# A fourth block of 32 rows in the stacked parts of x and B of the samples' state update

## The chip, the cores and the metric

The kernel runs on one core of one Trainium2 chip. A core has a matrix engine (TensorE; in profiles PE for its matmuls and PEld for its loads of the stationary operand), a vector engine (VectorE, DVE), a scalar engine (ScalarE, ACT), GpSimd (POOL) and a queue engine (SyncE, SP). They run side by side and wait for each other through semaphores. Matmuls write to PSUM, a small memory that VectorE and ScalarE empty. The metric is device time in microseconds, as the median of several runs.

## The reference

One decoder layer on a prompt of 1024 rows and on 8 samples of 8 rows each (64 rows), at model width 1024. What matters here is the recurrent branch of the samples. Each of the 8 samples has a state h for each of 32 heads, 64 x 128 numbers, which is decayed over its 8 rows and gets what these rows add:

```python
def step(h, inp):
    xq, dq, Bq, Cq = inp
    acs = jnp.cumsum(dq * Ag, axis=1)
    ...
    last = acs[:, -1]
    w_in = jnp.exp(last[:, None] - acs) * dq
    h = h * jnp.exp(last)[..., None, None] + jnp.einsum('bjgn,bjge,bjgep->bgepn', Bq, w_in, xq)
    return h, y
```

The sum over j runs over the 8 rows of a sample alone. Heads come in 4 groups of 8; B is shared within a group. All of it is float32.

## The kernel before

The kernel first normalises, then projects the 1088 rows to all columns, 128 columns at a time, with seven products for a pair of column blocks in place of eight (Strassen's scheme). In a product (`product`, L614) two halves of 272 rows are summed over 12 matmuls each; the first half goes to a PSUM buffer of the pool named mm or ps, the second to the other pool, in turn. There are three buffers mm, four buffers ps and one pc. The weights are split into a rounded high part and the rest: ScalarE makes `whi` (L165), GpSimd `wlo` (L168). Results are gathered in s, u and c: the first product of a pair is copied out of PSUM by ScalarE (L655, s<-mm and s<-ps), the others are added by VectorE (L623, L628, of which u<-s,mm and u<-s,ps at L623 start a new u). The finished sums go through an activation (L730, u<-u, with its table of functions loaded where the one before was another) and are stored to DRAM from ScalarE's queue (L732, for instance gp<-u); a new u reuses the buffer of the old one when its store has landed.

Between the last ten pairs of these projections the state work of the samples is done, written as the generator `all_samples` over the four head groups. For group g:

- `begin` loads the group's x, B and C of the samples (xb, tile hst) and the decay table (dec). `decay` masks dec on GpSimd (`far`, L1201 and L1202) and takes its exponentials on ScalarE (`exps`, L1207, eight instructions of 64 x 64).
- `rows` turns x and multiplies dec with C and B (L1255, L1257 on TensorE; L1259 and L1261 on VectorE).
- `spread` and `split` prepare one half hf of the samples (4 samples, 32 rows). `spread` copies the 32 columns of each of four x blocks and of B side by side, as often as there are blocks of 32 rows (`rep`, L1268, GpSimd). `split` turns them (L1279, L1281), so that 32 rows come out stacked several times, and makes of the stack parts of x and of B: x is weighted with wd3 (L1283) and rounded (L1288), and on rows 64:96 the rounded part is taken off the exact one (L1289); B is rounded (L1291), the rest stands on rows 32:64 (L1292), and the result is spread over four samples with the mask blk3 (L1293). Summed over the stack, the three blocks give high x high, high x low and low x high.
- `turn`, `turned` and `state` turn the old states (L1309, emptied by L1314 as hT and yt) and multiply them with C (L1323, on tiles of 32 columns).
- `update` sums over the stack, for two heads and four samples at once (L1332, 32 matmuls in all with 512 columns), and adds the decayed old state on VectorE (L1335); the new state is stored from ScalarE's queue (L1337, out<-h).
- `out` and `end` gather the samples' output (L1342, L1347, L1349, L1353) and store it (L1355, ys<-xd).

wd3 comes from a small product in `dt_end` (L1168, L1169) with a selector sel3 that repeats 32 rows (L1161).

The order of TensorE's instructions in this stage is kept as written (`in_line`). VectorE, ScalarE, GpSimd and SyncE get theirs from a scheduler that places instructions by its own costs; each engine then takes its queue strictly in that order, stores included. PSUM buffers are handed out in the same pass, so which operation frees the buffer that a product gets can change with the order.

Of the kernel before, what the change touches and what calls it, by code (L numbers as in the profile page):

```python
# [8 lines left out]
F32 = mybir.dt.float32  # L9
F32R = mybir.dt.float32r  # L10
AF = mybir.ActivationFunctionType
ALU = mybir.AluOpType
# [8 lines left out]
P = 128  # L21
# [4 lines left out]
NS = 64  # L26
T = SEQ + NS
DI = 2048
NH = 32
# [4 lines left out]
NC = SEQ // CH  # L34
# [12 lines left out]
def tile_pool_ssd_step(  # L47
# [6 lines left out]
    nc = tc.nc  # L54
    uid = [0]

    def nm(s):
        uid[0] += 1
        return f"{s}_{uid[0]}"
# [37 lines left out]
    def PB():  # L97
        return psB.tile([P, 512], F32, tag="ps", name=nm("ps"))

    def PA():  # L100
        return psA.tile([P, 512], F32, tag="mm", name=nm("mm"))
# [5 lines left out]
    def const(shape, name, dt=F32):  # L107
        return cp.tile(shape, dt, tag=name, name=name)
# [3 lines left out]
    mm = nc.tensor.matmul  # L112
    act = nc.scalar.activation
    V = nc.vector


    ident = const([P, P], "ident")
# [44 lines left out]
    def split(raw, kept=None, ncols=P, eng=None):  # L162
        hi = wp.tile([P, 4, P], F32R, tag="whi", name=nm("whi"), bufs=4)
        lo = wp.tile([P, 4, P], F32R, tag="wlo", name=nm("wlo"), bufs=4)
        ins = act(hi[:, :, :ncols], raw[:, :, :ncols], AF.Copy)  # L165
        if kept is not None:
            kept.append(ins.ins)
        (eng or nc.gpsimd).tensor_tensor(lo[:, :, :ncols], raw[:, :, :ncols], hi[:, :, :ncols].bitcast(F32), ALU.subtract)  # L168
        return hi, lo
# [4 lines left out]
    def prep(src, nk):  # L174
        out = []
        with tc.high_priority(PRI):
            for k0 in range(0, nk, 4):
                raw = raw_()
                load(raw, src[k0 * P:(k0 + 4) * P, :].rearrange("(k p) c -> p k c", p=P))
                out.append(split(raw))  # L180
        return out
# [347 lines left out]
    def pair_w(c0, c1, pri, early, second):  # L529
        def run():  # L530
# [9 lines left out]
            def add(x):  # L540
                with tc.high_priority(pri):
                    w.append(split(x, highs, eng=V if early else None))
# [326 lines left out]
    def first():  # L869
# [12 lines left out]
        def w_split(t, j, eng=None):  # L882
            w[t, j] = split(raws[t, j], eng=eng)
# [198 lines left out]
    def dt_end():  # L1082
# [4 lines left out]
        nc.gpsimd.affine_select(maskS, maskS, [[8, NB], [1, 8]], ALU.is_ge, 0.0, base=0, channel_multiplier=-1)  # L1087
        nc.gpsimd.affine_select(maskS, maskS, [[-8, NB], [0, 8]], ALU.is_ge, 0.0, base=0, channel_multiplier=1)
        nc.gpsimd.tensor_copy(blkS.rearrange("p (b i) -> p b i", i=8), blk.unsqueeze(2).to_broadcast([NS, NB, 8]))
        for rr in range(3):  # L1090
            nc.gpsimd.tensor_copy(blk3[32 * rr:32 * rr + 32], blk[:32, 0:4])
        F = 9 * NH
# [8 lines left out]
        def tmp(tag, bufs):  # L1101
            return sp.tile([P, 512], F32, tag=tag, name=nm(tag), bufs=bufs)[:, :F]
# [4 lines left out]
        for c0 in (0, 4, 8):  # L1107
            ps = PB()
# [3 lines left out]
            for c in cs:  # L1112
                n = P if c < 8 else NS
# [5 lines left out]
        r, e, q, s2, p = tmp("xd", 2), tmp("xw", 1), tmp("h0", H0B), tmp("h0", H0B), tmp("hT", 1)  # L1119
# [18 lines left out]
        a = q  # L1138
# [15 lines left out]
        for n, f in ((P, slice(0, 256)), (NS, slice(256, F))):  # L1154
# [1 line left out]
            V.tensor_tensor(wd[:n, f], pt[:n, f], ac[:n, f], ALU.subtract)  # L1156
            act(wd[:n, f], wd[:n, f], AF.Exp, scale=-1.0)
            V.tensor_tensor(wd[:n, f], wd[:n, f], dt[:n, f], ALU.mult)
        sel3 = sp.tile([NS, 2, 3, 32], F32, tag="hst", name="sel3", bufs=2)
        for hf in range(2):  # L1160
            nc.gpsimd.tensor_copy(sel3[:, hf], ident[:NS, 32 * hf:32 * hf + 32].unsqueeze(1).to_broadcast([NS, 3, 32]))  # L1161
        wdt = wdT[:NS, 8, :]
        act(Elb.rearrange("p c h -> p (c h)"), pt[:, :256], AF.Exp, scale=-1.0)
        yield
        yield
        ps = PB()
        for hf in range(2):
            mm(ps[:96, hf * NH:(hf + 1) * NH], sel3[:, hf].rearrange("p r i -> p (r i)"), wdt, start=True, stop=True)  # L1168
        V.tensor_copy(wd3.rearrange("p a h -> p (a h)"), ps[:96, :2 * NH])  # L1169
        for c0 in range(0, 9, 4):  # L1170
            cs = range(c0, min(c0 + 4, 9))
            n = sum(P if c < 8 else NS for c in cs)
            ps = PB()
# [51 lines left out]
    def spt(shape, tag, bufs, dt=F32):  # L1225
        return sp.tile(list(shape), dt, tag=tag, name=nm(tag), bufs=bufs)

    class Samples:
# [34 lines left out]
        def spread(self, hf):  # L1263

            xb = self.xb
            rep = spt([P, 5, 2, 3, 16], "xw", 1).rearrange("p q a r i -> p q (a r i)").rearrange(
                "p q (r i) -> p q r i", i=32)
            nc.gpsimd.tensor_copy(rep, xb[:, 0:5, 32 * hf:32 * hf + 32].unsqueeze(2).to_broadcast([P, 5, 3, 32]))  # L1268
            cz = spt([P, 4, 32], "cz", 2)
            V.memset(cz, 0.0)  # L1270
            V.tensor_copy(cz[:, :, 0:8], xb[:, 5, 32 * hf:32 * hf + 32].rearrange("p (b i) -> p b i", i=8))
            self.half[hf] = rep, cz

        def split(self, hf):
            g = self.g
            rep, cz = self.half[hf]
            px = PB()
            for q in range(4):
                nc.tensor.transpose(px[:96, q * P:(q + 1) * P], rep[:, q].rearrange("p r i -> p (r i)"), ident)  # L1279
            pb = PB()  # L1280
            nc.tensor.transpose(pb[:96, :P], rep[:, 4].rearrange("p r i -> p (r i)"), ident)  # L1281
            xs = spt([P, 8, 64], "xw", 1)
            V.tensor_tensor(xs[:96], px[:96].rearrange("p (h d) -> p h d", d=64),  # L1283
                            wd3[:, hf, 8 * g:8 * g + 8].unsqueeze(2).to_broadcast([96, 8, 64]), ALU.mult)
            both = spt([P, 2, 512], "dec", 2, F32R)
            xh, Bb = both[:, 0], both[:, 1].rearrange("p (b n) -> p b n", n=P)
            xsf = xs.rearrange("p h d -> p (h d)")
            act(xh[:96], xsf[:96], AF.Copy)  # L1288
            V.tensor_tensor(xh[64:96], xsf[64:96], xh[64:96].bitcast(F32), ALU.subtract)  # L1289
            bx = spt([P, P], "bt", 1, F32R)  # L1290
            act(bx[:96], pb[:96, :P], AF.Copy)  # L1291
            V.tensor_tensor(bx[32:64], pb[32:64, :P], bx[32:64].bitcast(F32), ALU.subtract)  # L1292
            V.tensor_tensor(Bb[:96], bx[:96].bitcast(F32).unsqueeze(1).to_broadcast([96, 4, P]),  # L1293
                            blk3.unsqueeze(2).to_broadcast([96, 4, P]), ALU.mult)
            self.half[hf] = xh, Bb, cz

        def within(self):
# [28 lines left out]
        def update(self, j):  # L1326

            g, (hf, r), E2 = self.g, divmod(j, 4), self.E2
            xh, Bb, cz = self.half[hf]
            h0 = self.h0.pop(j)  # L1330
            pu = PB()
            mm(pu, xh[:96, r * P:(r + 1) * P], Bb[:96].rearrange("p b n -> p (b n)"), start=True, stop=True)  # L1332
            for b in range(4):
                cc_ = 32 * hf + 8 * b + 7
                V.scalar_tensor_tensor(h0[:, b, :], h0[:, b, :], E2[:, r, cc_:cc_ + 1],  # L1335
                                       pu[:, b * P:(b + 1) * P], ALU.mult, ALU.add)
            store_(new_ssm_s[0, 4 * hf:4 * hf + 4, 8 * g + 2 * r:8 * g + 2 * r + 2]  # L1337
                   .rearrange("b h p n -> (h p) b n"), h0)
# [126 lines left out]
    hst = [None] * NG  # L1465
# [156 lines left out]
    def to_ssd():  # L1622
        nonlocal right, sd, sp, mask, maskS, blkS, dtT, acT, wdT, wd3, blk3, Elb
        right.__exit__(None, None, None)
        sd_cm = tc.tile_pool(name="sd", bufs=1, side="right", reuse_waits="tile")
        sd = sd_cm.__enter__()
        right_all.append(sd_cm)

        def one(shape, name):
            return sd.tile(shape, F32, tag=name, name=name, bufs=1)  # L1630
        mask, maskS, blkS = one([P, P], "mask"), one([NS, NB, 8], "maskS"), one([NS, NS], "blkS")
        dtT, acT, wdT = one([P, 9, NH], "dtT"), one([P, 9, NH], "acT"), one([P, 9, NH], "wdT")
        wd3, blk3, Elb = one([96, 2, NH], "wd3"), one([96, 4], "blk3"), one([P, NC, NH], "Elb")
        right = tc.tile_pool(name="sp", bufs=2, side="right", reuse_waits="tile")
        sp = right.__enter__()
        dt_steps.append(dt_end())
        next(dt_steps[0])
# [13 lines left out]
    pre = splits()  # L1651
    units.append(plain(lambda: [None for _ in pre]))
    units.append(plain(to_ssd))
    acc = [None] * 8
    yh, yl = [None] * NG, [None] * NG
# [234 lines left out]
    ps = PB()  # L1890
    for c in range(9):
        n = min(P, T - c * P)
# [5 lines left out]
    for c in range(9):  # L1898
        n = min(P, T - c * P)
# [144 lines left out]
    px, py, pz = PA(), PA(), PA()  # L2044
# [183 lines left out]
```

## Time and profile before

| what | value |
|---|---|
| runs | 1265.39, 1267.29, 1271.7 us |
| median of 3 | 1267.29 us |
| span of the profiled execution (first to last instruction; the only time given for it) | 1265.2 us |
| TensorE busy, matmuls / loads | 1239.8 us (98%) / 1158.1 us (92%) |
| VectorE, ScalarE, GpSimd busy | 77%, 54%, 57% |
| mean granted TensorE clock | 0.999 |
| TensorE's waits from 540 to 790 us, where the changed lines run | 2.0 us |

A row of a group in the profile reads: line, engine, operation, output<-inputs, shapes, count, then busy time in us and the mean duration of one in ns, then the engine's idle time just before these instructions and what ended it. For matmuls the shapes are rows*columns of the stationary operand and then the moving operand. In a timeline a row is start, duration, engine (a q behind it means its queue, for instance a DMA issue), line, operation, count, and in brackets the idle time ahead of it with its cause.

### The profile page before, as it was taken

How to read it: one execution, taken by the hardware profiler on the slowest of the kernel's cores; microseconds unless marked ns; L12 is line 12 of the kernel's file. 1: busy time of each engine (PE TensorE's matmuls, PEld its weight loads, DVE VectorE, ACT ScalarE, POOL GpSimd, SP SyncE). 2: the span in 40 equal slices, each digit the busy share in tenths (PEclk: the TensorE clock that was granted, in tenths of full speed). 3: DMA queues.
4: the chain of work that ended last, by engine and by line, in shares of the span. 5: the costliest groups of instructions: out<-in, count | busy, mean ns of one | idle time of the engine just before them, and what ended most of it. 6: DMA issues, size and time to landing. Idle time of an engine off the chain costs nothing.

```text
span 1265.2 us, 26432 instructions
## 1 busy us (share of the span) xinstructions
PE 1239.8 (98%) x9679; PEld 1158.1 (92%) x9679; DVE 974.4 (77%) x1713; ACT 682.6 (54%) x1566; POOL 716.2 (57%) x607
## 2 busy tenths in 40 slices
PE   7999999999999999999999999999999999999997
PEld 6779999999999999999999989998888988999886
DVE  4686689986998598876676775488677988759986
ACT  4665347465556546455656554646676656401425
POOL 1006767886968777764444444354686877503662
PEclk9999999999999999999999999999999999999999
DMA  9836554564546545444666565998878887866884
GB/s 328 265 112 205 152 158 155 180 205 157 162 154 199 160 155 176 131 150 122 175 177 194 166 178 154 324 308 274 253 241 288 279 250 247 275 226 219 250 192 158
DMA packets 262499, 257.99 MB, mean 204 GB/s; under 512 B 29761, under 2 KB 200337, under 8 KB 262362
## 3 DMA queue, kind: packets, MB, share of 16 engines
q1 hardware_dynamic: 181632, 163.93, 42.7%
q10 hardware_dynamic: 78434, 88.18, 20.2%
q0 software_dynamic: 2304, 4.20, 1.8%
q8 instruction: 77, 1.26, 0.4%
q14 instruction: 52, 0.43, 0.1%
HBM read 171.26 MB, written 85.10 MB: 203 GB/s over the span
## 4 chain that ended last, share of the span: by engine, by line
PE 65%; DMA 2%; DVE 2%; ACT 1%; issue 1%; POOL 0%; SPq 0%; ACTq 0%; DVEq 0%
PE mm L358 17%; PE mm L614 14%; PE ps L614 14%; PE ps L1219 3%; PE pc L614 2%; PE pc L1541 2%; PE ps L1222 2%; PE ps L2023 2%; PE ps L2025 2%; PE ps L2024 2%; PE ps L1309 1%; PE ps L1516 1%; PE ps L1332 1%; PE pc L1323 1%; PE mm L2033 1%
## 5 line engine op out<-in xcount | busy, mean ns | idle before, releaser
L168 POOL TENSOR_TENSOR wlo<-rawA,whi 128x512 fp32r<-128x512 f32 x120 | 174.2, 1456 | 175.2 <-ACT whi L165 89.8
L168 POOL TENSOR_TENSOR wlo<-raw,whi 128x512 fp32r<-128x512 f32 x92 | 153.2, 1674 | 106.9 <-ACT whi L165 75.3
L358 PE MATMUL mm<-Y,whi 128*128 128x352 f32 (+1 forms) x960 | 196.2, 334 | 0.3 <-DVE Y L1579 0.3
L358 PEld LDWEIGHTS mm<-Y,whi 128*128 128x128 f32 x960 | 159.1, 188 | 6.6 <-issue 5.1
L1062 DVE SCALAR_TENSOR_TENSOR GA<-GA,cvT,GA 128x1112 f32<-128x1112 f32 x72 | 133.4, 1857 | 0.1
L614 PE MATMUL mm<-Y,whi 128*128 128x272 f32 x832 | 125.3, 292 | 1.5 <-DVE Y L484 1.1
L614 PE MATMUL ps<-Y,whi 128*128 128x272 f32 x832 | 122.4, 289 | 0.0
L165 ACT ACTIVATE whi<-rawA 128x512 fp32r<-128x512 f32 x125 | 78.1, 627 | 76.0 <-PE ps L614 42.1
L165 ACT ACTIVATE whi<-raw 128x512 fp32r<-128x512 f32 x96 | 59.4, 628 | 106.4 <-DVE raw L546 48.4
L614 PEld LDWEIGHTS mm<-Y,whi 128*128 128x128 f32 x832 | 112.1, 188 | 4.8 <-DVE Y L484 1.5
L614 PEld LDWEIGHTS ps<-Y,whi 128*128 128x128 f32 x832 | 110.9, 188 | 0.4
L1207 ACT ACTIVATE dec<-dec,acT 128x128 f32<-128x128 f32 (+1 forms) x288 | 86.9, 383 | 27.0 <-POOL dec L1198 26.4
L358 PE MATMUL mm<-Y,wlo 128*128 128x352 f32 (+1 forms) x480 | 98.7, 327 | 0.0
L358 PEld LDWEIGHTS mm<-Y,wlo 128*128 128x128 f32 x480 | 81.7, 188 | 0.0
L434 POOL TENSOR_TENSOR pw<-pw,ph 128x512 fp32r<-128x512 f32 x40 | 68.4, 1711 | 12.6 <-ACT ph L432 11.5
L614 PE MATMUL mm<-G,whi 128*128 128x272 f32 x496 | 73.4, 289 | 0.0
L614 PE MATMUL ps<-G,whi 128*128 128x272 f32 x496 | 72.6, 288 | 0.0
L614 PE MATMUL mm<-Y,wlo 128*128 128x272 f32 x416 | 69.3, 288 | 0.0
L614 PE MATMUL ps<-Y,wlo 128*128 128x272 f32 x416 | 69.2, 288 | 0.0
L614 PEld LDWEIGHTS mm<-G,whi 128*128 128x128 f32 x496 | 66.6, 189 | 0.7
L614 PEld LDWEIGHTS ps<-G,whi 128*128 128x128 f32 x496 | 66.3, 188 | 0.0
L1478 POOL TENSOR_TENSOR Y<-xb,Y 128x512 fp32r<-128x512 f32 x32 | 41.7, 1304 | 37.0 <-ACT Y L1476 37.0
(531 smaller groups left out, 3192.5 us busy)
## 6 DMA issues: line engine op xcount, KB each, us to landing
rawA<-in_w_in SPq DMA_DIRECT2D x62, 512.0 KB
dec<-acs_d SPq DMA_DIRECT2D x32, 512.0 KB
xbc<-GA ACTq DMA_DIRECT2D x24, 512.0 KB
Y<-wo SPq DMA_DIRECT2D x10, 1024.0 KB
pw<-in_w_ssm_out ACTq DMA_DIRECT2D x32, 256.0 KB
ws<-ph ACTq DMA_DIRECT2D x32, 256.0 KB
ws<-pw ACTq DMA_DIRECT2D x32, 256.0 KB
h<-in_state_ssm SPq DMA_DIRECT2D x32, 256.0 KB
```

The costliest lines, as they stand in the source:

```text
L165: ins = act(hi[:, :, :ncols], raw[:, :, :ncols], AF.Copy)
L168: (eng or nc.gpsimd).tensor_tensor(lo[:, :, :ncols], raw[:, :, :ncols], hi[:, :, :ncols].bitcast(F32), ALU.subtract)
L358: mm(ps[:, :n], w[k // 4][h][:, k % 4, :], r[k][:, o:o + n], start=(j == 0), stop=(j == len(terms) - 1))
L434: nc.gpsimd.tensor_tensor(raw.bitcast(F32R), raw, hi.bitcast(F32), ALU.subtract)
L614: mm(p, w[j // 8][:, k], A(k, s)[j // 4 == 1], start=(j == 0), stop=(j == 11))
L1062: V.scalar_tensor_tensor(d[:, :n], rp[:, k:k + n], cvT[:, 24 * k + mc:24 * k + mc + 1], d[:, :n], ALU.mult, ALU.add)
L1207: act(dec[:, h], dec[:, h], AF.Exp, bias=acT[:S, c, 8 * g + h:8 * g + h + 1], scale=-1.0)
L1219: mm(o[hh], xd[:S, 2 * q + hh, :], dec[:S, 2 * q + hh], start=True, stop=state is None)
L1222: mm(o[hh], state[:, h * 64:h * 64 + 64], cE[:, h], start=False, stop=True)
L1478: nc.gpsimd.tensor_tensor(yl[g][:, :, o:o + S], v, yhc.bitcast(F32), ALU.subtract)
L1541: mm(pu, bt, xw.rearrange("p h d -> p (h d)"), start=True, stop=True)
L2023: mm(ps, hi, y[:, k, c0:c0 + cw], start=(first and k == 0), stop=False)
```

## The change

The stack gets a fourth block of 32 rows, so that 128 rows take part instead of 96. In B the block is zero, because its mask blk3 is set to zero first and only three blocks of it are filled; in x it holds one more rounded copy. The sum over the stack is therefore the same. `rep` and sel3 repeat four times instead of three; the turned blocks, the multiplications, casts and the product run over all 128 partitions; wd3 and blk3 have 128 rows.

```diff
+        nc.gpsimd.memset(blk3, 0.0)
         for rr in range(3):
             nc.gpsimd.tensor_copy(blk3[32 * rr:32 * rr + 32], blk[:32, 0:4])
...
-        sel3 = sp.tile([NS, 2, 3, 32], F32, tag="hst", name="sel3", bufs=2)
+        sel3 = sp.tile([NS, 2, 4, 32], F32, tag="hst", name="sel3", bufs=2)
...
-            mm(ps[:96, hf * NH:(hf + 1) * NH], sel3[:, hf].rearrange("p r i -> p (r i)"), wdt, start=True, stop=True)
-        V.tensor_copy(wd3.rearrange("p a h -> p (a h)"), ps[:96, :2 * NH])
+            mm(ps[:, hf * NH:(hf + 1) * NH], sel3[:, hf].rearrange("p r i -> p (r i)"), wdt, start=True, stop=True)
+        V.tensor_copy(wd3.rearrange("p a h -> p (a h)"), ps[:, :2 * NH])
...
-            rep = spt([P, 5, 2, 3, 16], "xw", 1).rearrange("p q a r i -> p q (a r i)").rearrange(
+            rep = spt([P, 5, 2, 4, 16], "xw", 1).rearrange("p q a r i -> p q (a r i)").rearrange(
                 "p q (r i) -> p q r i", i=32)
-            nc.gpsimd.tensor_copy(rep, xb[:, 0:5, 32 * hf:32 * hf + 32].unsqueeze(2).to_broadcast([P, 5, 3, 32]))
+            nc.gpsimd.tensor_copy(rep, xb[:, 0:5, 32 * hf:32 * hf + 32].unsqueeze(2).to_broadcast([P, 5, 4, 32]))
...
-                nc.tensor.transpose(px[:96, q * P:(q + 1) * P], rep[:, q].rearrange("p r i -> p (r i)"), ident)
+                nc.tensor.transpose(px[:, q * P:(q + 1) * P], rep[:, q].rearrange("p r i -> p (r i)"), ident)
...
-            act(xh[:96], xsf[:96], AF.Copy)
+            act(xh, xsf, AF.Copy)
...
-            act(bx[:96], pb[:96, :P], AF.Copy)
+            act(bx, pb[:, :P], AF.Copy)
...
-            V.tensor_tensor(Bb[:96], bx[:96].bitcast(F32).unsqueeze(1).to_broadcast([96, 4, P]),
-                            blk3.unsqueeze(2).to_broadcast([96, 4, P]), ALU.mult)
+            V.tensor_tensor(Bb, bx.bitcast(F32).unsqueeze(1).to_broadcast([P, 4, P]),
+                            blk3.unsqueeze(2).to_broadcast([P, 4, P]), ALU.mult)
...
-            mm(pu, xh[:96, r * P:(r + 1) * P], Bb[:96].rearrange("p b n -> p (b n)"), start=True, stop=True)
+            mm(pu, xh[:, r * P:(r + 1) * P], Bb.rearrange("p b n -> p (b n)"), start=True, stop=True)
...
-        wd3, blk3, Elb = one([96, 2, NH], "wd3"), one([96, 4], "blk3"), one([P, NC, NH], "Elb")
+        wd3, blk3, Elb = one([P, 2, NH], "wd3"), one([P, 4], "blk3"), one([P, NC, NH], "Elb")
```

Behind the memset all lines move down by one in the changed kernel (L1332 is L1333 there).

More of the change, by code (lines that the diff above doesn't have):

```diff
@@ L1158, in dt_end @@
             V.tensor_tensor(wd[:n, f], wd[:n, f], dt[:n, f], ALU.mult)
-        sel3 = sp.tile([NS, 2, 3, 32], F32, tag="hst", name="sel3", bufs=2)
+        sel3 = sp.tile([NS, 2, 4, 32], F32, tag="hst", name="sel3", bufs=2)
         for hf in range(2):
-            nc.gpsimd.tensor_copy(sel3[:, hf], ident[:NS, 32 * hf:32 * hf + 32].unsqueeze(1).to_broadcast([NS, 3, 32]))
+            nc.gpsimd.tensor_copy(sel3[:, hf], ident[:NS, 32 * hf:32 * hf + 32].unsqueeze(1).to_broadcast([NS, 4, 32]))
         wdt = wdT[:NS, 8, :]
@@ L1278, in split @@
             for q in range(4):
-                nc.tensor.transpose(px[:96, q * P:(q + 1) * P], rep[:, q].rearrange("p r i -> p (r i)"), ident)
+                nc.tensor.transpose(px[:, q * P:(q + 1) * P], rep[:, q].rearrange("p r i -> p (r i)"), ident)
             pb = PB()
-            nc.tensor.transpose(pb[:96, :P], rep[:, 4].rearrange("p r i -> p (r i)"), ident)
+            nc.tensor.transpose(pb[:, :P], rep[:, 4].rearrange("p r i -> p (r i)"), ident)
             xs = spt([P, 8, 64], "xw", 1)
-            V.tensor_tensor(xs[:96], px[:96].rearrange("p (h d) -> p h d", d=64),
-                            wd3[:, hf, 8 * g:8 * g + 8].unsqueeze(2).to_broadcast([96, 8, 64]), ALU.mult)
+            V.tensor_tensor(xs, px.rearrange("p (h d) -> p h d", d=64),
+                            wd3[:, hf, 8 * g:8 * g + 8].unsqueeze(2).to_broadcast([P, 8, 64]), ALU.mult)
             both = spt([P, 2, 512], "dec", 2, F32R)
```

## The prediction

> **What bounds the kernel now.** I read the page first, then TensorE's waits in the stage that the change touches, then the rows by shape, then the timeline of two short stretches. The page:
>
> ```profile
> span 1265.2 us, 26432 instructions
> PE 1239.8 (98%) x9679; PEld 1158.1 (92%) x9679; DVE 974.4 (77%) x1713; ACT 682.6 (54%) x1566; POOL 716.2 (57%) x607
> PE 65%; DMA 2%; DVE 2%; ACT 1%; issue 1%; POOL 0%; SPq 0%; ACTq 0%; DVEq 0%
> ```
>
> TensorE runs for 98% of the span and carries the chain of waits, so only what lengthens a matmul or makes TensorE stand still counts; the other engines matter through the waits they cause. All that the diff edits runs between 545 and 790 us, and from 540 to 790 us the view of waits has one entry for TensorE (total, times, longest):
>
> ```profile
> PE ps L1332 <- ACT s L655: 2.0, 2, 1.7
> ```
>
> That is the edited product itself, held twice by ScalarE's copy s (L655), which empties a PSUM buffer that the product wants.
>
> **The change part by part.** Rows by shape (count, busy us, mean ns, idle before):
>
> ```profile
> L1332 PE MATMUL ps<-dec 96*128 96x512 f32 x32 | 12.2, 452 | 2.0 <-ACT s L655 2.0
> L2023 PE MATMUL ps<-Y,s3h 128*128 128x512 f32 x20 | 7.9, 396 | 0.0
> L1332 PEld LDWEIGHTS ps<-dec 96*128 96x128 f32 x32 | 4.9, 187 | 5.8 <-issue 2.8 <-ACT s L655 2.6 <-DVE xd L1259 0.4
> L2023 PEld LDWEIGHTS ps<-Y,s3h 128*128 128x128 f32 x28 | 5.3, 188 | 0.9
> L1279 PEld LDWEIGHTS ps<-ident,xw 128*96 128x96 f32 x32 | 3.6, 126 | 0.0
> L1309 PEld LDWEIGHTS ps<-ident,h 128*128 128x128 f32 x128 | 14.5, 141 | 0.0
> L1283 DVE TENSOR_TENSOR xw<-ps,wd 96x512 f32<-96x512 f32 x8 | 5.5, 682 | 0.6 <-PE ps L1281 0.6
> L1527 DVE TENSOR_TENSOR xd<-ps,dtT 128x512 f32<-128x512 f32 x32 | 21.8, 681 | 6.0 <-PE ps L1516 6.0
> L1288 ACT ACTIVATE dec<-xw 96x512 fp32r<-96x512 f32 x8 | 5.0, 628 | 4.1 <-DVE xw L1283 4.1
> L165 ACT ACTIVATE whi<-rawA 128x512 fp32r<-128x512 f32 x125 | 78.1, 627 | 76.0 <-PE ps L614 42.1
> L1268 POOL COPY xw<-hst 128x480 f32<-128x480 f32 x8 | 4.7, 586 | 26.6 <-DVE dec L1289 12.9 <-PE ps L614 7.4 <-PE ps L1309 3.2
> L1161 POOL COPY sel<-ident 64x96 f32<-64x96 f32 x2 | 0.5, 258 | 0.0
> ```
>
> The 32 products of L1332: load 187 ns at 96 rows, 188 at 128. The matmul's mean is 452 against 396 ns at 128 rows. If rows caused that, the change would save 32 x 56 = 1.8 us; if they cost in proportion, 32 x 452/3 = 4.8 us. I take 0, the value of the loads: in the timeline rows below a product lasts 0.49 us behind the column-tiled L1323, so by the mean the one behind it is left 2 x 452 - 490 = 414 ns, near the 396. The excess belongs to the place, and L1323 stays.
>
> The 40 transposes (L1279, L1281) load 128 columns instead of 96: 141 - 126 = 15 ns each, 0.6 us as the upper end, 0 as the lower; I take 0, since their idle is 0.0 and the load lies beside the matmul before it. Without that cover it is the 0.6. The four loads for wd (L1168) go with them.
>
> VectorE and ScalarE take the same time on 96 and 128 partitions (682 and 681 ns, 628 and 627): nothing for the multiplications, the casts and the copy of wd3. The correction on rows 64:96 and that on 32:64 are unchanged.
>
> POOL's eight copies `rep` grow from 480 to 640 elements. From 258 ns at 96 to 586 at 480 is 0.85 ns an element, so 137 ns more each, 1.1 us in all; sel3 (32 elements more, twice) and the new memset of blk3 (below 258 ns) add at most 0.4. POOL stood 26.6 us before these copies and TensorE never waited for them. The cover is TensorE's work between copy and transpose; if it were gone, 1.5 us.
>
> **The order moves.** TensorE's order in this stage is written down and stays. That of ScalarE is chosen by a scheduler, and in the changed program it differs at two places, where group 1 and group 3 of the samples take over from the group before:
>
> ```
> before: table, exp x7, store out, exp, store out, whi, table, u x2, store gp<-u, s<-mm, whi, s<-ps
> after:  store out, store out, whi, table, exp x8, table, u x2, s<-mm, whi, s<-ps, store gp<-u
> ```
>
> And the PSUM buffers swap: the second L1332 of the pair now waits for VectorE instead of ScalarE, and the second half of the next projection product (L614, ps<-Y) waits for ScalarE's s<-ps instead. The second place before, ScalarE, then VectorE and TensorE (start, duration):
>
> ```profile
> 726.19 1.28 ACT L1207 ACT_TABLE_LOAD   x1
> 727.49 1.78 ACT L1207 ACTIVATE dec<-dec,acT 64x64 f32<-64x64 f32 x7
> 729.36 0.40 ACTq L1337 DMA_DIRECT2D out<-h  x1
> ...
> 730.39 0.40 ACTq L1337 DMA_DIRECT2D out<-h  x1
> 730.89 0.63 ACT L165 ACTIVATE whi<-rawA 128x512 fp32r<-128x512 f32 x1 [0.74 <-DVE u L628]
> 731.54 1.28 ACT L730 ACT_TABLE_LOAD   x1
> 732.83 0.75 ACT L730 ACTIVATE u<-u 128x272 f32<-128x272 f32 x2
> 733.61 0.34 ACTq L732 DMA_DIRECT2D gp<-u  x1
> 734.06 0.40 ACT L655 ACTIVATE s<-mm 128x272 f32<-128x272 f32 x1 [0.48 <-PE ps L1332]
> ...
> 734.88 0.39 ACT L655 ACTIVATE s<-ps 128x272 f32<-128x272 f32 x1
> ```
>
> ```profile
> 737.48 0.44 DVE L623 TENSOR_TENSOR u<-s,mm 128x272 f32<-128x272 f32 x1 [0.41 <-DMA gp<-u]
> 733.09 0.49 PE L1332 MATMUL ps<-dec 96*128 96x512 f32 x1
> 735.32 0.50 PE L1332 MATMUL ps<-dec 96*128 96x512 f32 x1 [1.73 <-ACT s L655]
> 735.65 1.16 PE L614 MATMUL mm<-Y,whi 128*128 128x272 f32 x8
> 737.15 1.16 PE L614 MATMUL ps<-Y,whi 128*128 128x272 f32 x8
> 739.96 0.60 PE L1279 MATMUL ps<-ident,xw 128*96 128x128 f32 x4
> 741.21 1.28 PE L614 MATMUL mm<-Y,whi 128*128 128x272 f32 x8
> 741.16 0.60 ACT L1314 ACTIVATE yt<-ps 128x512 f32<-128x512 f32 x1 [0.78 <-PE ps L1281]
> ```
>
> Before, the exponentials fill the time in which the stores wait for VectorE's updates of h. After, the two stores stand first, ScalarE waits behind them until 730.8, and whi starts at 730.89 as before. Only then come table (1.28), eight exp (1.78 + 0.25 = 2.03), table (1.28) and u x2 (0.75): 731.54 + 5.34 = 736.9. From s<-mm to the end of s<-ps took 734.06 to 735.27, 1.21: the end is now 738.1, 2.8 later.
>
> TensorE: the exponentials end at 734.86, VectorE's multiplication of dec behind them (about 0.7, the length of its 512 columns) frees the second L1332's buffer at 735.6, so it starts about 0.3 later than 735.32 and the old wait brings no gain. The ps half would be due 1.8 later (737.15 - 735.32), at 737.4, but its buffer comes at 738.1 plus 0.05: a start of 738.15 instead of 737.15, **1.0 us lost**.
>
> Next in line is the store gp<-u. It goes out when u is done, 736.9 instead of 733.61, and VectorE's L623 overwrites its source: it started 737.48 - 733.61 = 3.87 us behind the issue. So it comes to 740.8, and VectorE takes its queue in order: the second L623 follows 0.35 later and ends at 741.6. L1279 waits for VectorE; by the round of four buffers I take the one that this L623 empties. Due at 739.96 + 1.0 = 740.96, it starts at 741.65: another 0.7, **1.7 us at this place**.
>
> The first place, the same steps:
>
> ```profile
> 641.02 0.40 ACTq L1337 DMA_DIRECT2D out<-h  x1
> 644.52 0.34 ACTq L732 DMA_DIRECT2D gp<-u  x1
> 645.78 0.39 ACT L655 ACTIVATE s<-ps 128x272 f32<-128x272 f32 x1
> 648.33 0.44 DVE L623 TENSOR_TENSOR u<-s,mm 128x272 f32<-128x272 f32 x1
> 648.08 1.16 PE L614 MATMUL ps<-Y,whi 128*128 128x272 f32 x8
> 650.88 0.60 PE L1279 MATMUL ps<-ident,xw 128*96 128x128 f32 x4
> ```
>
> whi can start at 641.02 + 0.40 + 0.10 = 641.5; with 0.63 + 5.34 u ends at 647.5 and s<-ps at 648.7 (646.17 before). ps<-Y starts at 648.75 instead of 648.08: 0.65. gp<-u leaves at 647.55, L623 comes 3.81 later, 651.36, the second ends at 652.15, and L1279 starts at 652.2 instead of 650.88: **1.3 us**.
>
> The sum is 1.3 + 1.7 = 3.0 us. Apart from these places TensorE's queue holds the same work in the same order, so a delay moves everything behind it and is not won back. On the profiled span that is 1268.2; the median of the runs before, 1267.29, lies 2.1 above that span, so I put the sum on the median: **1270.3 us**. Against the bound, 0.5% or 6.3 us (about what a measurement of this kernel can tell from no change), it is no change.
>
> **The rivals.** First, the cure works: the second L1332 is free of ScalarE, and the 2.6 us that its loads waited for s shrink by the two 0.2 us that any L1332 pair pays. That needs s<-ps of the second place to end when ps<-Y is due after an early second product (one behind the first at 733.09 + 0.49, so 735.4), 0.1 later than now; I work out 2.8 later, and dec's multiplication bars the early start. It gives 1265.1, 2.2 faster.
>
> Second, a drain goes. From the rows: the loads of L1332 stood 2.8 us for "issue", and if 96 rows caused it, 128 would save 2.8, to 1264.5. L2023's 128 rows show little idle, but nothing column-tiled stands ahead of them. The Trainium skill, "TensorEngine Tiling", section "Key Properties", says that changing the tiling mode drains TensorE; its list knows no 96-row mode, and by it the drain would belong to L1323.
>
> Third, the reorder is covered: either VectorE has freed another buffer for L1279 (only 0.65 + 1.0 is lost, 1268.9), or s<-ps is not that late (1267.3).
>
> Fourth, the lateness spreads. VectorE's queue behind L623 ends 3 us later. ScalarE's store of ys waits for that queue, and behind the store stands yt, which empties PSUM ahead of the next ps half. At its old distance yt ends at 741.16 + 0.60 + 1.7 = 743.5, and that half is due 1.5 (737.15 - 735.65) behind its mm half, at 741.21 + 1.5 + 1.7 = 744.4: a cover of 0.9 us. Overrun by 1 to 2 us at each place, it gives 5 to 7 us: 1272.3 to 1274.3 and, with the copies' and loads' 2.1 uncovered as well, 1276.4.
>
> **How the numbers follow.** The forecast 0.55; rivals in order 0.07, 0.03, 0.20, 0.15. The runs before reach from 1265.39 to 1271.7, which takes the forecast to 1268 to 1274. The range goes down to 1264.5, the second rival, and up to 1276.5, the fourth; of the 2 in 10 outside, most lies above. Slower by over 0.5% (above 1273.6) takes most of the fourth case and the upper end of the forecast, 0.18; faster (below 1261) needs both gains at once or an odd set of runs, 0.04; the rest, 0.78, is within.
>
> **What would show it.** The wait of L1332 for s gone from the view of waits, and L614 ps waiting for ACT s L655 twice instead, 0.7 to 3 us each; a wait of DVE u L623 for the store gp<-u of about 3 us twice; L1279 waiting for DVE. L1332's mean near 452 ns, loads of L1279 near 141, `rep` near 723. It is wrong if L1332's matmul shortens or lengthens with rows, if no L614 waits for s, or if the sum of TensorE's waits in this stage is not 3 us above the 2.0 of before.

## The result and the profile after

The changed kernel takes 1272.52 us (median of 22 runs, 1269.53 to 1275.74) against 1269.89 us for the kernel before on the same chip (22 runs, 1265.01 to 1275.07). The ratio is 1.0028, with an interval of 1.0017 to 1.0039: 2.2 to 5.0 us slower, less than the 0.5% taken as the bound. The two medians lie 2.6 us apart.

The page of the changed kernel (its lines stand one lower in the code):

```profile
span 1273.3 us, 26425 instructions
PE 1245.1 (98%) x9679; PEld 1163.4 (91%) x9679; DVE 973.9 (76%) x1713; ACT 682.7 (54%) x1566; POOL 718.7 (56%) x608
PE 65%; DVE 2%; DMA 2%; issue 1%; ACT 1%; POOL 1%; SPq 0%; ACTq 0%; DVEq 0%; POOLq 0%
```

TensorE still carries everything. Its waits from 540 to 800 us, and then two of VectorE's between 630 and 760 us (total, times, longest):

```profile
PE ps L614 <- ACT s L655: 5.1, 2, 2.6
```

```profile
DVE dec L1262 <- ACT dec L1208: 3.4, 2, 1.7
DVE u L623 <- DMA gp<-u: 2.8, 2, 1.4
```

The wait of the edited product (L1332, now L1333) for s is gone, and the second half of the next projection product waits for s instead, twice, 2.56 us each. That is 3.1 us more than the 2.0 of before. The rows by shape, and for the transposes' loads the view of their line (shortest, median and longest ns):

```profile
L614 PE MATMUL ps<-Y,whi 128*128 128x272 f32 x832 | 123.0, 290 | 5.1 <-ACT s L655 5.1
L1333 PE MATMUL ps<-dec 128*128 128x512 f32 x32 | 11.6, 445 | 0.0
L1333 PEld LDWEIGHTS ps<-dec 128*128 128x128 f32 x32 | 4.8, 188 | 3.2 <-issue 2.8 <-DVE xd L1260 0.4
L1269 POOL COPY xw<-hst 128x640 f32<-128x640 f32 x8 | 5.7, 717 | 29.2 <-DVE dec L1290 15.4 <-PE ps L614 7.4 <-PE ps L1310 3.2
L1284 DVE TENSOR_TENSOR xw<-ps,wd 128x512 f32<-128x512 f32 x8 | 5.5, 686 | 3.4 <-PE ps L1282 3.4
```

```profile
L1280 PEld LDWEIGHTS ps<-ident,xw x32: 138/141/231, 603.5 to 772.8; 128*128 128x128 f32 x32
```

The product's load lasts 188 ns (187 before), its matmul 445 (452), so 128 rows are no dearer than 96. The first place where a group takes over, ScalarE and then TensorE:

```profile
643.79 1.43 ACTq L1338 DMA_DIRECT2D out<-h  x2
645.35 0.63 ACT L165 ACTIVATE whi<-rawA 128x512 fp32r<-128x512 f32 x1 [4.50 <-DVE u L628]
646.00 1.28 ACT L1208 ACT_TABLE_LOAD   x1
647.29 2.02 ACT L1208 ACTIVATE dec<-dec,acT 64x64 f32<-64x64 f32 x8
649.33 1.28 ACT L730 ACT_TABLE_LOAD   x1
650.62 0.75 ACT L730 ACTIVATE u<-u 128x272 f32<-128x272 f32 x2
651.40 0.34 ACTq L732 DMA_DIRECT2D gp<-u  x1
652.08 0.39 ACT L655 ACTIVATE s<-ps 128x272 f32<-128x272 f32 x1
```

```profile
647.75 0.73 PE L1333 MATMUL ps<-dec 128*128 128x512 f32 x2
648.31 1.15 PE L614 MATMUL mm<-Y,whi 128*128 128x272 f32 x8
652.51 1.62 PE L614 MATMUL ps<-Y,whi 128*128 128x272 f32 x8 [2.56 <-ACT s L655]
657.03 0.60 PE L1280 MATMUL ps<-ident,xw 128*128 128x128 f32 x4
...
743.99 1.26 PE L614 MATMUL ps<-Y,whi 128*128 128x272 f32 x8 [2.56 <-ACT s L655]
```

ScalarE stands idle 4.50 us behind its two stores; the exponentials, which filled that time before, come after it, and s<-ps ends at 652.47. TensorE starts 0.04 us later.

The matmuls behind the wait are also slower: eight of L614 take 1.62 us, not 1.15. Busy time by window (window, length, TensorE, its loads, VectorE, ScalarE, GpSimd, then the granted clock):

```profile
649.82:653.23 3.41, 0.85 (x7) 0.72 (x6) 2.44 (x11) 3.12 (x7) 0.98 (x1) 1.00 0.31 104
653.23:656.64 3.41, 3.41 (x18) 3.41 (x17) 1.52 (x4) 0.63 (x1) 1.58 (x2) 0.50 0.73 163
656.64:660.05 3.41, 3.41 (x40) 3.17 (x39) 1.67 (x3) 2.95 (x8) 0.00 (x0) 1.00 0.94 257
745.39:748.80 3.41, 3.41 (x18) 3.41 (x18) 1.25 (x4) 1.44 (x3) 1.27 (x1) 0.50 0.72 161
```

Behind each of the two standstills the clock is halved for 3.41 us. The profiled execution of before had a clock of 1.00 all through this stage.

Set against the trace of before by the start of every matmul, TensorE loses 2.7 us to the wait and 1.7 to the clock at each of the two places, and gains 0.5 and 2.0 where the second product no longer waits: 6.3 us in this stage (an expectation below puts this at 6.2 and a half-clock stretch at 1.5). Of the other 1.8 us between the two spans (1273.3 and 1265.2), 2.1 arise before 105 us, where another half-clock stretch at 55.9 us falls in this execution, and 0.3 are won later. That stretch is in both traces of the changed kernel and in neither of the kernel before, but also in traces with the order of before (at 56.1 us in that of the order kept, at 55.7 and 55.2 us in two of the kernel before with its stores moved). So this pair of profiles shows more than the medians do; the runs below say why.

### The profile page after: what moved, and what is told of

The parts are those of the page before. It is cut to its first block, busy times and chain, and to the rows that moved or that the text cites. A ratio compares the mean times of both kernels' runs of the same rounds, so it can differ in the third digit from the quotient of the medians.

```text
span 1273.3 us, 26425 instructions
## 1 busy us (share of the span) xinstructions
PE 1245.1 (98%) x9679; PEld 1163.4 (91%) x9679; DVE 973.9 (76%) x1713; ACT 682.7 (54%) x1566; POOL 718.7 (56%) x608
## 4 chain that ended last, share of the span: by engine, by line
PE 65%; DVE 2%; DMA 2%; issue 1%; ACT 1%; POOL 1%; SPq 0%; ACTq 0%; DVEq 0%; POOLq 0%
PE mm L358 17%; PE ps L614 14%; PE mm L614 13%; PE ps L1220 2%; PE pc L614 2%; PE pc L1542 2%; PE ps L1223 2%; PE ps L2024 2%; PE ps L2026 2%; PE ps L2025 2%; DMA xb<-xbc 1%; PE ps L1310 1%; PE ps L1517 1%; DVE h L1336 1%; PE ps L1333 1%
## 5 line engine op out<-in xcount | busy, mean ns | idle before, releaser
L168 POOL TENSOR_TENSOR wlo<-rawA,whi 128x512 fp32r<-128x512 f32 x120 | 173.7, 1452 | 182.8 <-ACT whi L165 95.2
L168 POOL TENSOR_TENSOR wlo<-raw,whi 128x512 fp32r<-128x512 f32 x92 | 152.7, 1670 | 104.6 <-ACT whi L165 70.7
L614 PE MATMUL ps<-Y,whi 128*128 128x272 f32 x832 | 123.0, 290 | 5.1 <-ACT s L655 5.1
L614 PE MATMUL mm<-Y,whi 128*128 128x272 f32 x832 | 125.2, 292 | 1.8 <-ACT whi L165 1.0
L614 PEld LDWEIGHTS mm<-Y,whi 128*128 128x128 f32 x832 | 112.1, 188 | 5.3 <-ACT whi L165 1.4
L614 PEld LDWEIGHTS ps<-Y,whi 128*128 128x128 f32 x832 | 111.1, 188 | 5.9 <-ACT s L655 5.6
L614 PE MATMUL mm<-G,whi 128*128 128x272 f32 x496 | 73.4, 289 | 0.0
L614 PE MATMUL ps<-G,whi 128*128 128x272 f32 x496 | 72.6, 288 | 0.0
L614 PE MATMUL ps<-Y,wlo 128*128 128x272 f32 x416 | 69.9, 290 | 0.0
L614 PE MATMUL mm<-Y,wlo 128*128 128x272 f32 x416 | 69.3, 288 | 0.0
L614 PEld LDWEIGHTS mm<-G,whi 128*128 128x128 f32 x496 | 66.7, 189 | 0.7
L614 PEld LDWEIGHTS ps<-G,whi 128*128 128x128 f32 x496 | 66.3, 188 | 0.0
```

The source lines that it names most:

```text
L614: mm(p, w[j // 8][:, k], A(k, s)[j // 4 == 1], start=(j == 0), stop=(j == 11))
```

## The experiments

Two theories stood against each other: ScalarE's order costs the time (the exponentials behind something that comes late), or the 128 rows and the longer copy do. One thing more moves with ScalarE's order, in every run that has the new one: at both places GpSimd runs a second `wlo` (L168) ahead of the second mask of dec (L1202). No run separates this from ScalarE's order.

**The rows without the longer copy.** Here `rep` stays 480 elements long, VectorE clears 32 columns behind it, and each transpose reads 128 adjoining columns; the fourth block then holds other numbers, which meet the zeros in B. ScalarE's order is that of the kernel before.

```diff
-            nc.gpsimd.tensor_copy(rep, xb[:, 0:5, ...].to_broadcast([P, 5, 4, 32]))
+            flat = spt([P, 8, 64], "xw", 1).rearrange("p h d -> p (h d)")
+            rep = flat[:, :480].rearrange("p (q r i) -> p q r i", q=5, i=32)
+            V.memset(flat[:, 480:], 0.0)
+            nc.gpsimd.tensor_copy(rep, xb[:, 0:5, ...].to_broadcast([P, 5, 3, 32]))
...
-            self.half[hf] = rep, cz
+            self.half[hf] = flat, cz
...
-                nc.tensor.transpose(px[:, q * P:(q + 1) * P], rep[:, q]..., ident)
+                nc.tensor.transpose(px[:, q * P:(q + 1) * P], rep[:, 96 * q:96 * q + P], ident)
```

> All work of the change on 128 rows, but GpSimd copies only the 480 elements of before (the transposes read 128 adjoining columns of them, and VectorE clears 32 columns, eight more instructions of below 0.17 us). ScalarE's order is again that of before. Order theory (the rows cost nothing, the loss is ScalarE's order at the two places): ratio to before 0.999 to 1.001, no L614 waiting for ACT s L655, the product of the update waiting for s about 2 us in all as before, granted clock 1.00 between 640 and 760 us. Rows theory (128 rows cost TensorE or the others time): ratio 1.002 to 1.004, and the order does not matter.

1270.28 us against 1268.68, ratio 1.0003 (0.9985 to 1.0021). TensorE's waits in the stage:

```profile
PE ps L1334 <- ACT s L655: 1.9, 2, 1.6
```

The wait is the old one, at the old place. All matmuls, casts and multiplications over 128 rows cost nothing that shows within the interval (1.9 us faster to 2.7 slower).

**The longer copy alone.** 96 rows everywhere, but `rep` is written four times over and the transposes read three blocks of it. ScalarE's order is that of the changed kernel.

```diff
-            nc.gpsimd.tensor_copy(rep, xb[:, 0:5, ...].to_broadcast([P, 5, 3, 32]))
+            nc.gpsimd.tensor_copy(rep, xb[:, 0:5, ...].to_broadcast([P, 5, 4, 32]))
...
-                nc.tensor.transpose(px[:96, ...], rep[:, q]..., ident)
+                nc.tensor.transpose(px[:96, ...], rep[:, q, 0:3]..., ident)
```

> The kernel before with one part of the change: GpSimd's copy has 640 elements, the fourth block is never read, everything else stays at 96 rows. ScalarE's order becomes that of the changed kernel. Order theory: ratio to before 1.002 to 1.004 like the changed kernel, L614 ps waiting for ACT s L655 twice, 2.5 us each, TensorE's clock at half for about 3.4 us behind each wait. Rows theory: ratio 0.999 to 1.001, no such waits.

1271.22 us against the same 1268.68, ratio 1.0016 (0.9993 to 1.0039). TensorE at the two places:

```profile
652.21 1.66 PE L614 MATMUL ps<-Y,whi 128*128 128x272 f32 x8 [3.47 <-ACT s L655]
742.30 1.27 PE L614 MATMUL ps<-Y,whi 128*128 128x272 f32 x8 [1.10 <-ACT s L655]
```

The new waits come without a single further row in the product. The time alone decides nothing (the interval holds 1.000), the rows of the trace do. That the two waits differ so much, 3.47 and 1.10, was new.

**The change in full, with the order kept.** GpSimd copies three blocks as before, and VectorE the fourth in an instruction of its own. The result is the same as with the change; ScalarE's order is that of before.

```diff
-            nc.gpsimd.tensor_copy(rep, xb[:, 0:5, ...].to_broadcast([P, 5, 4, 32]))
+            nc.gpsimd.tensor_copy(rep[:, :, 0:3], xb[:, 0:5, ...].to_broadcast([P, 5, 3, 32]))
+            V.tensor_copy(rep[:, :, 3], xb[:, 0:5, ...])
```

> The change in full (128 rows, rep four times over, the same result), but the fourth block of rep is copied by VectorE in an instruction of its own, so GpSimd's copy keeps its 480 elements; ScalarE's order is then that of the kernel before. If only ScalarE's order costs time, this is the kernel before: a median within 1.5 us of it, TensorE waiting at L1334 (before: L1332) for ScalarE's s for 2 to 3.2 us in all and never at L614 ps. If the 128 rows cost time in themselves, the median lies 3 to 4 us above the kernel before, as that of the changed kernel does.

1267.91 us against 1268.07, ratio 0.9994 (0.9978 to 1.001), and the old wait:

```profile
PE ps L1334 <- ACT s L655: 2.0, 2, 1.7
```

This settles the main question: with the order put back, the work of the change is free within 0.2%, and the interval lies below that of the changed kernel (1.0017 to 1.0039). What the change costs, it costs through the order. The one part that this run leaves out is GpSimd's longer copy; the run before this one has it without the rows, and TensorE waits for the copy neither there nor in the changed kernel.

**Both kernels once more.** One further execution each.

> The changed kernel once more, to see what repeats in its profile. If a standstill of 2.56 us halves the clock by itself, L614 ps waits 2.5 to 2.6 us for ScalarE's s twice and a stretch of 3.4 us at half the clock follows each time, near 653 and 745 us; if the stretches fall by chance, one or both are missing or lie elsewhere. The stretch near 56 us, seen in some executions of both kernels, may or may not be there.

> The kernel before once more. If standstills set the half-clock stretches, none lies between 600 and 800 us, where its waits are 0.3 and 1.7 us; if they fall by chance, they may. TensorE's waits between 540 and 790 us should be 2.0 us again, within 0.3.

The changed kernel, its waits, and the clock in the steps around the second standstill:

```profile
PE ps L614 <- ACT s L655: 5.2, 2, 2.6
```

```profile
738.83:742.24 3.41, 2.39 (x26) 1.91 (x14) 1.67 (x7) 3.38 (x10) 0.00 (x0) 1.00 0.52 149
742.24:745.65 3.41, 1.83 (x15) 1.84 (x16) 1.76 (x7) 2.47 (x7) 1.28 (x1) 1.00 0.47 159
745.65:749.06 3.41, 3.41 (x41) 3.18 (x40) 2.57 (x6) 1.90 (x6) 1.27 (x1) 1.00 0.91 206
```

The kernel before, the same two views:

```profile
PE ps L1332 <- ACT s L655: 3.2, 2, 1.6
```

```profile
644.44:647.85 3.41, 1.76 (x23) 1.14 (x23) 2.38 (x7) 2.85 (x7) 1.23 (x2) 1.00 0.66 197
647.85:651.26 3.41, 3.41 (x17) 3.41 (x17) 1.65 (x6) 0.00 (x0) 0.52 (x1) 0.50 0.87 243
```

The first expectation missed in part, the second in both its points. The changed kernel waited 2.63 and 2.60 us, but the clock fell only behind the first. The kernel before waited 3.2 us and not 2.0, and its clock fell too, behind a wait of 1.65 us. So the kernel before is not always as quick as its first profile, and the difference between the kernels is smaller than those two profiles make it.

Why the waits differ stands in VectorE's rows just ahead of the stores. Its sum L546 (rawA) in the first profile of before, at the first place, elsewhere, and at the second place; then in that of the changed kernel:

```profile
636.53 2.39 DVE L546 TENSOR_TENSOR rawA<-rawA,rawA 128x512 f32<-128x512 f32 x1
666.94 0.68 DVE L546 TENSOR_TENSOR rawA<-rawA,rawA 128x512 f32<-128x512 f32 x1
...
724.14 4.15 DVE L546 TENSOR_TENSOR rawA<-rawA,rawA 128x512 f32<-128x512 f32 x1
```

```profile
638.81 3.92 DVE L546 TENSOR_TENSOR rawA<-rawA,rawA 128x512 f32<-128x512 f32 x1
...
730.28 3.92 DVE L546 TENSOR_TENSOR rawA<-rawA,rawA 128x512 f32<-128x512 f32 x1
```

The sum lasts 0.68 us at 666.94 and 1.1 to 5.1 at the takeovers of the 14 traces, where GpSimd runs one instruction after the other beside it. GpSimd beside the sum at 724.14:

```profile
725.39 1.10 POOL L1202 TENSOR_SCALAR_AFFINE_SELECT dec<-dec 64x512 f32<-64x512 f32 x1
726.46 1.28 POOL L168 TENSOR_TENSOR wlo<-raw,whi 128x512 fp32r<-128x512 f32 x1
727.71 1.74 POOL L546 TENSOR_TENSOR raw<-raw,rawA 128x512 f32<-128x512 f32 x1
```

The sum ends at 728.29, 0.55 us behind the end of L168 at 727.74, and the GpSimd instruction that then runs takes 1.74 us. The updates of h come behind the sum, and ScalarE's stores wait for them. From the timelines of seven executions (first and second place, us):

| kernel | ScalarE's order | sum L546 | TensorE's wait for s |
|---|---|---|---|
| before | before | 2.39, 4.15 | 0.25, 1.73 |
| before, once more | before | 4.07, 3.94 | 1.65, 1.53 |
| rows without the copy | before | 4.05, 2.60 | 1.64, 0.26 |
| change, order kept | before | 4.16, 1.33 | 1.75, 0.26 |
| copy alone | after | 4.86, 2.49 | 3.47, 1.10 |
| after | after | 3.92, 3.92 | 2.56, 2.56 |
| after, once more | after | 3.99, 3.95 | 2.63, 2.60 |

In the order of before the wait is the sum's time less 2.41 (4.15 - 1.73 = 2.42, 4.07 - 1.65 = 2.42, 4.05 - 1.64 = 2.41), and not under 0.25. In the order of after it is the sum's time less 1.35 to 1.39. So where the sum takes more than about 2.7 us, the order of after costs 1.0 us more at each place; at shorter sums it costs less, because the wait of before does not go below 0.25.

**Other work in the standstill.** The changed kernel with 20 discarded matmuls ahead of the mm half of the two products concerned.

```diff
-            for j in range(12):
-                k = j % 4
-                mm(p, w[j // 8][:, k], A(k, s)[j // 4 == 1], start=(j == 0), stop=(j == 11))
+            for n in (8, 12, 12) if turn[0] in FILL else (12,):
+                for j in range(n):
+                    k = j % 4
+                    mm(p, w[j // 8][:, k], A(k, s)[j // 4 == 1], start=(j == 0), stop=(j == n - 1))
```

> The changed kernel with 20 more matmuls of 272 columns (their sums are overwritten) in the two stretches in which TensorE stood still for 2.56 us: eight and twelve ahead of the last twelve of the mm half. Clock theory (the standstill makes the clock fall to half for 3.4 us, 1.5 us lost each time): the extra work is free, the clock stays at 1.00 there, and the profiled loss of 6.2 us in this stage becomes about 3.1; ratio to before 1.000 to 1.002. Rival (the clock falls for another cause, or does not cost the runs anything): half clock stays, ratio as for the changed kernel, 1.002 to 1.004. If the wait were not idle for TensorE, the 20 matmuls would cost 2.5 us at each place, ratio above 1.005.

1272.57 us, ratio 1.0031 (1.0013 to 1.0048): no gain. Its waits, and the windows behind the two places:

```profile
PE ps L615 <- ACT s L657: 0.8, 1, 0.8
```

```profile
650.00:654.00 4.00, 4.00 (x46) 3.77 (x45) 2.70 (x5) 1.38 (x3) 1.28 (x1) 1.00 1.01 266
742.00:746.00 4.00, 4.00 (x46) 3.77 (x45) 3.04 (x6) 2.44 (x8) 1.28 (x1) 1.00 1.06 269
```

The waits that are left are 0.8 us, and the clock stays at 1.00. Over its 12 runs the mean granted clock is 0.9970, against 0.9954 over the 22 of the changed kernel. But the 20 matmuls last 2.5 us each time, whether VectorE's sum has made the wait that long or not: in this execution the sums took 2.53 and 4.61 us, so by the rule above 1.2 and 3.2 us were there to be filled. What the clock gave back, the filling took. That the half clock comes from TensorE standing still is borne out (the last section has the counts over all traces); that time is won by a filling of fixed length is refuted.

**Moving the stores.** In the kernel before, the six stores of updates 4 and 5 ahead of a takeover go to SyncE's queue (`load` issues there):

```diff
-            store_(new_ssm_s[0, 4 * hf:4 * hf + 4, ...], h0)
+            (load if j in (4, 5) and g < 3 else store_)(new_ssm_s[0, 4 * hf:4 * hf + 4, ...], h0)
```

> The kernel before, with the two stores of new states that stand among the exponentials (updates 4 and 5 of groups 0 to 2) issued from SyncE's queue. Order theory: ScalarE runs the eight exponentials without a stop, s of the second place comes 1.3 us earlier, the product waits 0.4 instead of 1.7 us for it; ratio 0.998 to 1.000. Rival: loads queue behind these stores on SyncE's queue and something waits for weights or states, ratio above 1.001.

1267.05 us against 1268.68, ratio 0.998 (0.9964 to 0.9996); TensorE's waits in the stage:

```profile
PE ps L1332 <- ACT s L655: 0.7, 2, 0.5
```

The time met the expectation. The trace alone does not show what the stores do, since the sum L546 took only 1.23 and 1.25 us in it, and at such sums the kernel before would wait no longer. The same edit in the changed kernel:

> All of the changed kernel's work (128 rows, the copy of 640 elements), with the samples' state stores of updates 4 and 5 of groups 0 to 2 issued on SyncE's queue, so that they no longer stand in ScalarE's queue. If rows and copy cost nothing and only the place of these stores does, the 2.6 us waits of L614 ps for ScalarE's s shrink to under 1 us each, no half-clock stretch follows them, and the median is within 1 us of that of the kernel before with the same stores moved (1267.0): 1266.5 to 1268.5, below the changed kernel's 1272.5. If rows or copy cost time of their own, or if the rest of the order matters and not the stores, it stays at 1270 or above.

1272.86 us against 1269.26, ratio 1.0029 (1.001 to 1.0048): a miss. Waits and the timeline of ScalarE say why:

```profile
PE ps L1333 <- ACT s L655: 4.0, 2, 2.0
```

```profile
642.75 0.63 ACT L165 ACTIVATE whi<-rawA 128x512 fp32r<-128x512 f32 x1 [2.24 <-PE ps L614]
643.40 1.28 ACT L1208 ACT_TABLE_LOAD   x1
```

The stores are gone, but `whi` still stands in front of the exponentials, and it waits for TensorE's product, 2.24 us at both places. TensorE's two waits are 2.0 us each, though the sums took 2.53 and 3.82 us, so here the sum does not set them. It is not the stores as such that hurt, but anything that comes late ahead of the exponentials. The expectation had named only the stores and the rows; it was the rest of the order.

All state stores on SyncE's queue, first in the kernel before (`load` for every j and g), then in the kernel with 128 rows and the order kept:

> The kernel before with all stores of the updated states (L1337) on SyncE's queue, also those that stand ahead of no exponentials. If a store that waits for VectorE holds up ScalarE anywhere else on TensorE's path, this is faster than with the six stores moved alone (1267.0 against 1268.7 for the kernel before): 1265 to 1266.5. If only the two takeovers matter, it is the same, 1266.5 to 1267.5. If the loads on SyncE's queue are now held up behind waiting stores, it is slower than 1268.7.

> The same, with all stores of the updated states on SyncE's queue. If the rows cost nothing, it takes what the kernel before takes with the same stores moved, 1265.1 within 1.5 us, and so beats the kernel before; waits of L1334 for s 0.5 us in all. If the rows cost time, 1268 or more.

The first took 1265.11 us against 1269.26, ratio 0.9972 (0.9957 to 0.9986), the second 1267.84 against 1268.07, ratio 0.9998 (0.9981 to 1.0014), above the 1266.6 at which its expectation ended. The profiles of the two showed no cause for a difference: the waits are alike (the kernel before, then that with 128 rows), and the spans are 1263.8 and 1263.6 us, though the second profile is of its fastest run.

```profile
PE ps L1332 <- ACT s L655: 0.5, 2, 0.2
```

```profile
PE ps L1334 <- ACT s L655: 0.5, 2, 0.3
```

In the second the sums took 3.97 and 4.64 us, for which the rule of the order of before gives waits of 1.6 and 2.2 us; they are 0.23 and 0.30. With the stores out of ScalarE's queue, the sum no longer reaches TensorE.

So both ran once more, side by side:

> The kernel before with all state stores on SyncE's queue once more, beside its counterpart with 128 rows. If its first reading (0.9972 of the time before) holds, 1264.5 to 1266.5 against about 1268.5 for the kernel before; if that was chance, within 1 us of the kernel before.

> The same stores moved in the kernel with 128 rows and ScalarE's order kept, once more. If 128 rows cost nothing, the two kernels lie within 1 us of each other here; if rows or VectorE's extra copies cost what separated them before, this one is 2 to 3 us slower.

1266.29 us, ratio 0.9972 (0.9954 to 0.999), and 1267.44 us, ratio 0.9979 (0.9962 to 0.9997), against 1270.2. They lie 1.15 us apart, a little over the 1 us expected, and their intervals overlap almost wholly. In their traces TensorE waits 0.4 us in the stage in the first, and 0.8 for s and 0.5 for a load of a state in the second. Whether 128 rows with the copies on VectorE still cost a microsecond here stays open. The kernel before with all its state stores on SyncE's queue beats both kernels of this study in both readings, by 0.28% against the kernel before.

## Why the prediction was right, and where its steps were not

The forecast was 3.0 us, no change by the bound; the ratio makes it 3.5 (2.2 to 5.0), the medians 2.6. The 1270.3 itself lies 2.2 below the 1272.52, because it stood on 1267.29, the median of 3 runs, where the 22 runs have 1269.89.

- **128 rows cost nothing on TensorE:** right. Loads of 188 ns and matmuls of 445 were foreseen as 188 and 452, the transposes' loads at 141, and the change with the order kept gives 0.9994 (0.9978 to 1.001). The excess of the 452 belonged to the place, as said.
- **The copies on GpSimd, hidden:** right, 717 ns against 723; no wait of TensorE for them.
- **The order moves the wait from L1332 to L614 ps:** right, and TensorE's loss in this stage lies there and in the clock behind it. The time of s<-ps at the second place was right to 0.1 us too (743.94, less the 5.93 us by which `whi` starts later than in the trace of before, is 738.0; forecast 738.1).
- **The second L1333 held back by dec's multiplication:** wrong. The two run as a pair at 647.75 with no wait, while the exponentials end at 649.31 and the multiplication comes behind them. So the buffer was free earlier; which instruction frees it the views do not show. This shifts where TensorE waits more than how long in sum: at the second place the new wait is longer (2.56 instead of 1.0) and the old one is won back (1.73), which leaves 0.8 against the forecast 1.0.
- **0.65 at the first place:** near for the execution that it was read from, too small in general. It rested on one trace in which VectorE's sum happened to take 2.39 us; by the rule above 2.39 - 1.37 - 0.25 = 0.8. In six of the seven executions of the table the sum takes 3.9 us or more there, and then the place costs 1.0.
- **L1279 waits for VectorE's L623, 0.65 and 0.7:** wrong. The step that failed took 3.8 us, the distance of L623 from the store before, for the store's landing. In the trace of before L623 adds TensorE's mm half, which ended only at 737.32, 0.16 us ahead of it, so the distance was not the store's, although the row names the store. In the changed kernel L623 follows 2.3 us behind the issue at 651.40:

```profile
653.69 0.44 DVE L623 TENSOR_TENSOR u<-s,mm 128x272 f32<-128x272 f32 x1 [1.43 <-DMA gp<-u]
655.15 0.44 DVE L623 TENSOR_TENSOR u<-s,ps 128x272 f32<-128x272 f32 x1 [1.03 <-PE ps L614]
```

  L623 waited 1.43 us for the store, not 3, and its second part ended 1.4 us ahead of L1280 at 657.03. The 1.3 us are not there.
- **In their place, the clock:** not foreseen. A half-clock stretch costs 1.7 us. In the 104 runs of the kernel before beside the experiments the mean granted clock is 0.9962; in the 22 of the changed kernel it is 0.9954. One stretch takes 3.41 x 0.5 / 1270 = 0.0013 off the mean, so by estimate the changed kernel has about 0.6 more of them in an execution: 1.0 us. This is not firm. The four sets that make up the 104 runs lie between 0.9958 and 0.9966, and the 128 rows without the copy, with the order of before, had 0.9956.

So the sum was right and its terms were not. In the table TensorE waits 2.3 us an execution in the order of before and 5.0 in that of after, 2.7 more, instead of the forecast 1.65. At the sums seen in the order of before, the rule above gives about 1.7 of this to ScalarE's order; the rest comes from longer sums, by chance or by GpSimd's moved order, which no run separates. With the clock's estimate of 1.0 in place of the 1.3 for L1279 that makes 3.7, where the times show 2.6 to 3.5. That the forecast of 3.0 lies in the midst of these is luck.

Of the rivals the third was right in the mechanism of its first branch: L1280 did not wait for VectorE. Its 1.65 us was still too low, since the waits for s were longer and the clock came on top. The others did not come true: the loads of the product stand 2.8 us for issue with 128 rows as with 96, so no drain hung on the rows, and TensorE has no wait for yt, so the lateness did not spread that way.

## What to carry to other kernels

An engine that takes its queue in order should have nothing that comes late in front of work that is ready and on whose end TensorE depends. Here two stores, or one cast, ahead of eight exponentials kept TensorE waiting, while a third more rows in 32 products was free. When a small change lets a scheduler choose anew, compare the queues first, and to judge the change itself, make it once with the old order kept. A wait read in one execution can hang on one instruction whose time differs from execution to execution: look at a second execution before a term of a sum rests on it.

## What the runs showed of the hardware

**The clock is granted in fixed steps.** Apart from the last one of each trace, which runs into the end, every half-clock stretch in the 14 traces lasts 3.413 us, and within a trace the stretches start whole numbers of 3.4133 us apart (in the changed kernel 55.90, 653.23 and 745.39 us: 175.0 and 202.0 steps). What counts is how much of a standstill falls into one step. Leaving out the first and the last 20 us of each trace: with more than 1.85 us of a step idle, the next was at half clock 9 times of 9; with 1.4 to 1.8 us, 7 times of 16; below that never, except near 1120 us in three traces, where no such standstill is recorded. That fits the two waits of 2.6 us in one execution that differed: the one at 741.22 was cut by a step's end at 742.24 into 1.02 and 1.58 us. The Trainium skill, "TensorE: Matmul & The Clock Gate", section "What's actually happening", says that the clock is gated by a free-running window of 3413 ns; the traces agree. Its table there gives half clock after at least one idle window of about 3.4 us; here half a window was enough, and the measurement decides. Why the steps between 1.4 and 1.8 us split was not tried.

**VectorE's sum beside GpSimd.** A sum of two SBUF operands of 128 x 512 took 0.68 us where no GpSimd instruction ran beside it, and 1.1 to 5.1 us at the 28 takeovers of the 14 traces. The long ones come in steps: each of the 28 ended 0.47 to 0.64 us behind the end of a GpSimd instruction, the first, second, third or fourth end since its start, and in 27 of them the GpSimd instruction that then ran was 0.35 to 0.55 us longer than elsewhere. So the sum gets through only where one GpSimd instruction ends and the next begins. A sum that starts at such an end takes 0.68 us although GpSimd is busy throughout, as at 666.94 in the trace of before. Which of the ends a sum gets differed from execution to execution, and why was not tried. The Trainium skill, "GPSIMD Engine Reference", section "1. Specifications", says that GpSimd shares its SBUF interfaces with VectorE, with contention for instructions with two SBUF inputs; the trace agrees with that. It is the source of the spread in these waits.
